# A trunk layer on one core: the first four column tiles take the input without its norm

## The chip, the core and the metric

The kernel runs on one core of one Trainium2 chip. The core has a matrix engine (TensorE, "PE" in the profile, with its weight loads as "PEld"), a vector engine (VectorE, "DVE"), a scalar engine that applies functions (ScalarE, "ACT"), GpSimd ("POOL") and a queue that issues the transfers (SyncE, "SP"). Each engine works through its own list of instructions in order, and waits where an instruction needs what another engine or a transfer has not yet delivered. The metric is the device time of one execution in microseconds (us); lower is better.

## What is computed

One layer works on 640 tokens of 1024 channels: 128 context tokens and 512 latent tokens. The part that the change touches is the first sub-layer's input:

```python
sh1, sc1, g1, sh2, sc2, g2 = split(silu(cond) @ w_ada + b_ada)      # per channel; cond: c_ctx for context, c for latent
h    = rmsnorm(x, norm1_g) * (1 + sc1) + sh1
proj = h @ w_in + b_in                                              # q, k, v, o, gates, u, ga, gb
```

`rmsnorm` multiplies each token by the reciprocal root of its mean square over the channels. The columns of `proj` feed a bidirectional mLSTM (q, k, v, o and the gate columns), a convolution branch (u, through a gated linear unit) and two branch gates; both branches are merged and projected, and a second sub-layer (norm, gated MLP with a depthwise convolution) and a final norm follow. All in float32.

## The kernel before

Activations lie transposed: channels on the 128 partitions, the 640 tokens along the free axis, so x is 8 tiles of 128x640 (index j). A column tile of `proj` is 128 output columns by 640 tokens and sums over the 8 channel tiles. For precision each float32 product is taken as three fast ones (`three`): every operand is split into a rounded high part and the rest, and high x high, low x high, high x low are summed in PSUM. Weights come in groups of 8 blocks of 128x128 (tile `wst`, 512 KB). ACT rounds such a group to `wh`, DVE subtracts to get `wl`. For the activations ACT makes `hh` and DVE makes `hl`.

The start runs like this. The 8 x tiles are loaded, then `ada1` weights (tiles `adst`, 16 loads of 512 KB) alternate with weight groups. ACT squares each x tile (`sq`), and PE sums the squares over the partitions (`colsum_into`, into a `ps` tile). `rstd` makes the reciprocal root (`rsy`), and `bcast` spreads it by PE over the partitions (kept as `rbs`). For each j the task `ada1` lets PE multiply the modulation weights with the condition (`ps<-adst,sc_pad`), ACT copies the row (`mrow`), PE turns it to columns (`ps<-sel,mrow`), and DVE makes the shift `mods` and the scale `a1`. The task `first_h(j)` then does, for tile j: on DVE x times `rbs`; on ACT `hh` = scale and shift of x, rounded; on DVE the same scale and shift in place; on DVE `hl`, the difference.

The first four column tiles (`FIRST`: two of u, the gate columns "g", the first of k) are computed together, j in the outer loop, so that a tile j can be used as soon as it is ready: 32 groups of three products, each over 256 and 384 tokens. Their sums occupy two `mm` tiles and two `ps` tiles of PSUM. After them come single tiles (`mtile`), beginning with q 0, k 1, q 1, u 1, each needing `hh` and `hl` of all 8 j. There are two `mm` tiles, so the third such tile needs the first one evicted.

Behind the first tiles ACT evicts: `gy` and `gt` (the gated unit), `gi` and `az` (the mLSTM's gates), `k`. DVE then runs the gates' scans (`bc`, `M`) and makes `pk` and `mj`, which PE transposes in the midst of tile u 1. The weights of the convolution (31 taps per tile, DVE), and later the modulation of the second sub-layer, are DVE work that is filled in wherever a place is free.

The order of each engine's list is set when the program is built: a small planner (`_Order`) keeps an estimated time for each engine, runs a task's next step when its inputs are estimated as ready, and so interleaves tasks (`od.spawn`, `yield`, `od.until`). On the chip the lists are fixed. All operations go through one helper, so every row of the profile has the same line, and one tells them apart by tile names.

## Time and profile before

| | |
|---|---|
| Time, median of 3 runs | 977.38 us (976.42 to 977.95) |
| The profiled execution's own time | 975.71 us |
| Its span (first to last instruction) | 973.5 us |
| PE busy | 946.8 us, 97% |
| DVE busy | 735.1 us, 76% |
| ACT busy | 362.2 us, 37% |
| POOL busy | 6.0 us, 1% |
| First matmul of the column tiles starts | 21.54 us |
| Last matmul of the first four tiles starts | 61.34 us |

A row of the timeline gives the start in us, the busy time in us, the engine, the operation with output and inputs by tile name and shapes, the number merged, and in brackets the idle time of the engine just before and who ended it. A row of the groups gives the count, the busy time in us and the mean of one in ns, and the idle time before. A row of the windows gives, for a stretch, the busy time (and count) of PE, PEld, DVE, ACT and POOL, then the granted TensorE clock, the busy share of the transfer engines, and GB/s.

### The profile page before, as it was taken

The page shows a single profiled execution, that of the slowest core. Times are in us where ns is not written, and L with a number is a line of the kernel's source. Part 1 is how long each engine was busy: PE and PEld are TensorE (multiplying, and loading weights), DVE is VectorE, ACT ScalarE, POOL GpSimd, SP SyncE. Part 2 cuts the span into 40 slices and gives each one's busy share as a digit, 9 for nine tenths or more (in the row PEclk, how much of TensorE's full clock was granted, in tenths as well). Part 3 has the DMA queues.
Part 4 walks back from the last instruction along what each step waited for, and adds up shares of the span by engine and source line. Part 5 has one row for each costly group of instructions (what it writes and reads, how often), then busy time and mean ns, then how long its engine had stood idle before and what let it go on. Part 6 is the DMA issues. An engine that isn't in the chain of part 4 may idle for free.

```text
span 973.5 us, 16460 instructions
## 1 busy us (share of the span) xinstructions
PE 946.8 (97%) x6700; PEld 924.2 (95%) x6700; DVE 735.1 (76%) x1348; ACT 362.2 (37%) x658; POOL 6.0 (1%) x41
## 2 busy tenths in 40 slices
...
GB/s 355 245 104 87 45 76 66 74 47 45 87 141 71 104 196 189 201 233 251 147 135 102 77 79 63 163 87 65 82 71 65 88 68 84 65 88 94 123 170 113
DMA packets 38971, 113.01 MB, mean 116 GB/s; under 512 B 4336, under 2 KB 7280, under 8 KB 38896
## 3 DMA queue, kind: packets, MB, share of 16 engines
...
q8 instruction: 53, 0.87, 0.4%
...
## 4 chain that ended last, share of the span: by engine, by line
PE 92%; DVE 4%; ACT 2%; issue 1%; DMA 1%; SPq 0%; DVEq 0%; ACTq 0%
PE mm L139 84%; PE ps L139 8%; DVE junk L139 1%; DVE acc L139 1%; DMA x<-in_xT 1%; DVE wl L139 0%; ACT wh L139 0%; ACT h L139 0%; ACT L139 0%; DVE rsy L139 0%; DVE yo L139 0%; ACT h2h L139 0%; DVE rst L139 0%; ACT sq L139 0%; SPq L139 0%
## 5 line engine op out<-in xcount | busy, mean ns | idle before, releaser
L139 ACT ACTIVATE wh<-wst 128x1024 fp32r<-128x1024 f32 x145 | 152.9, 1057 | 197.1 <-PE mm L139 166.8
L139 DVE TENSOR_TENSOR wl<-wst,wh 128x1024 fp32r<-128x1024 f32 x145 | 176.5, 1220 | 56.2 <-ACT wh L139 55.9
L139 PE MATMUL mm<-h2h,wl 128*128 128x320 f32 x704 | 164.9, 310 | 2.4 <-DVE wl L139 2.4
L139 PE MATMUL mm<-h2h,wh 128*128 128x320 f32 x704 | 165.0, 310 | 0.6 <-ACT h2h L139 0.6
L139 PE MATMUL mm<-h2l,wh 128*128 128x320 f32 x704 | 164.8, 310 | 0.4 <-DVE h2l L139 0.4
L139 PE MATMUL mm<-hh,wh 128*128 128x320 f32 (+2 forms) x576 | 134.3, 312 | 3.5 <-ACT wh L139 2.5
L139 PE MATMUL mm<-hl,wh 128*128 128x320 f32 (+2 forms) x576 | 133.7, 311 | 0.0
L139 PE MATMUL mm<-hh,wl 128*128 128x320 f32 (+2 forms) x576 | 133.4, 310 | 0.0
L139 DVE SCALAR_TENSOR_TENSOR acc<-gbuf,cols,acc 128x455 f32<-128x455 f32 (+2 forms) x176 | 129.7, 742 | 4.4
L139 PEld LDWEIGHTS mm<-h2h,wl 128*128 128x128 f32 x704 | 119.2, 189 | 2.8 <-DVE wl L139 2.7
L139 PEld LDWEIGHTS mm<-h2h,wh 128*128 128x128 f32 x704 | 119.3, 189 | 1.3 <-ACT h2h L139 1.2
L139 PEld LDWEIGHTS mm<-h2l,wh 128*128 128x128 f32 x704 | 119.1, 188 | 1.1 <-DVE h2l L139 1.0
L139 DVE SCALAR_TENSOR_TENSOR z<-glu,cols,z 128x641 f32<-128x641 f32 (+14 forms) x120 | 102.2, 889 | 0.8
L139 PEld LDWEIGHTS mm<-hh,wh 128*128 128x128 f32 x576 | 96.0, 188 | 5.8 <-ACT wh L139 3.0
L139 PEld LDWEIGHTS mm<-hl,wh 128*128 128x128 f32 x576 | 96.6, 188 | 2.2 <-issue 1.3
L139 PEld LDWEIGHTS mm<-hh,wl 128*128 128x128 f32 x576 | 96.9, 189 | 0.7 <-issue 0.7
L139 PE MATMUL mm<-ah,wl 128*128 128x320 f32 (+2 forms) x320 | 85.6, 308 | 0.0
L139 PE MATMUL mm<-ah,wh 128*128 128x320 f32 (+2 forms) x320 | 85.4, 307 | 0.0
L139 PE MATMUL mm<-al,wh 128*128 128x320 f32 (+2 forms) x320 | 85.4, 307 | 0.0
L139 DVE SCALAR_TENSOR_TENSOR junk<-ad,cb 128x512 bf16<-128x512 f32 x128 | 81.8, 686 | 0.1
L139 PEld LDWEIGHTS mm<-ah,wl 128*128 128x128 f32 x320 | 56.8, 188 | 0.1
L139 PEld LDWEIGHTS mm<-al,wh 128*128 128x128 f32 x320 | 56.8, 188 | 0.0
...
## 6 DMA issues: line engine op xcount, KB each, us to landing
wst<-in_w SPq DMA_DIRECT2D x145, 512.0 KB, 3.6
...
adst<-in_ada SPq DMA_DIRECT2D x16, 512.0 KB, 10.2
x<-in_xT SPq DMA_DIRECT2D x16, 320.0 KB, 5.7
...
```

The lines of the kernel that those rows point to most:

```text
L139: return fn(*args, **kw)
```

## The change

The first four column tiles no longer take the normed input. A new task `scaled(j)` makes, as soon as x tile j and its modulation are there, g = x times `a1` (scale only, no norm), with two columns more that hold the shift of both conditions (642 columns), and splits it: `gh` on ACT, `gl` on DVE (a ring of 6 tiles, `NFG`). `FIRST` is computed on g. When the sums leave PSUM, `first_out` multiplies them on DVE with `rbs` (the norm is one factor per token, so it may be applied behind the product) into an SBUF tile `fo`, copies the two columns that the shift gave (`fs`), and adds those on ACT. The tiles that follow read `fo` in place of PSUM.

The normed input for all other tiles is made by a task `normed`: for each j on DVE g times `rbs` in place, on ACT `hh` = g plus the shift, rounded, on DVE the shift added in place, on DVE `hl`. The sum of squares is a task `norm1`: ACT squares, GpSimd adds the eight tiles up, PE sums once over the partitions (4 matmuls where there were 32). The loads go by turns: `cols`, modulation weights of j = 0, x 0, `sel`, a weight group, x 1, and so on; the bytes are the same.

The lists move as follows. PE at its start (`sq` are squares, `adst` modulation weights, `rsy` the norm, `mm` the first tiles); before:

```order
L139 MATMUL ps<-sq,ones_83 32x160 x32
L139 MATMUL ps<-adst,sc_pad 32x256 x8
L139 MATMUL ps<-rsy,sel 128x160 x4
L139 MATMUL ps<-sel,mrow 128x128 x2
L139 MATMUL ps<-adst,sc_pad 32x256 x8
L139 MATMUL mm<-hh,wh 128x256
```

and now:

```order
L140 MATMUL ps<-adst,sc_pad 32x256 x8
L140 MATMUL ps<-sel,mrow 128x128 x2
L140 MATMUL mm<-gh,wh 128x256
L140 MATMUL mm<-gh,wh 128x386
L140 MATMUL mm<-gl,wh 128x256
L140 MATMUL mm<-gl,wh 128x386
L140 MATMUL mm<-gh,wl 128x256
L140 MATMUL mm<-gh,wl 128x386
L140 MATMUL ps<-adst,sc_pad 32x256 x8
```

The sums of squares and the broadcast of the norm, which stood ahead of the first tile, have gone behind its beginning; one modulation product stands ahead of it instead of two.

DVE around the normed input, in the part of the first four tiles; before (tile j, then the next, with the modulation and a weight group between):

```order
L139 TENSOR_TENSOR x<-x,rbs 128x640 [waits DMAHW6_49]
L139 TENSOR_SCALAR x<-x,a_211,mods 128x128 [waits Activation_49]
L139 TENSOR_SCALAR x<-x,a_211,mods 128x512 [waits Activation_49]
L139 TENSOR_TENSOR hl<-x,hh 128x640 [waits DVE_49]
```

and now, beginning with the weights of j = 4 and 5 (each row with what it waits for):

```order
L140 TENSOR_TENSOR wl<-wst,wh 128x1024 [waits DMAHW2_49]
L140 TENSOR_TENSOR g<-g,rbs 128x640
L140 TENSOR_SCALAR g<-g,mods 128x128 [waits Activation_49]
L140 TENSOR_SCALAR g<-g,mods 128x512 [waits Activation_49]
L140 TENSOR_TENSOR hl<-g,hh 128x640 [waits DVE_49]
L140 TENSOR_SCALAR a_156<-ps,sc1p,cols 128x2 [waits PE_49]
L140 TENSOR_SCALAR mods<-ps,cols 128x2
L140 TENSOR_SCALAR g<-x,a_156 128x128 [waits DMAHW3_49,DVE_49]
L140 TENSOR_SCALAR g<-x,a_156 128x512
L140 COPY g<-mods 128x2 [waits DVE_49]
L140 TENSOR_TENSOR gl<-g,gh 128x642 [waits DVE_49,PE_49,Activation_49]
L140 TENSOR_TENSOR wl<-wst,wh 128x1024 [waits DMAHW5_49]
```

Here normed tile 0 stands ahead of the modulation and of `gl` for j = 7 and of the weights for j = 6 and 7; three weight groups, normed tiles 1 and 2, the twelve rows that take the four tiles out of PSUM (`fo`, `fs`) and then normed tiles 3 to 7 follow, four rows each, one tile behind the other.

ACT where the evictions of the first tiles begin; before:

```order
L139 ACTIVATE wh<-wst 128x1024 [waits DMAHW7_49,PE_49,Activation_49]
L139 ACTIVATE gy<-mm,halfc 128x256 [waits PE_49]
L139 ACTIVATE gy<-mm,halfc 128x384
L139 ACT_TABLE_LOAD
L139 ACTIVATE gt<-mm,halfc 128x256
```

and now:

```order
L140 ACTIVATE fo<-fo,fs 128x512
L140 ACTIVATE hh<-g,mods 128x128 [waits DVE_49,Pool_49]
L140 ACTIVATE hh<-g,mods 128x512
L140 ACTIVATE gy<-fo,halfc 128x640 [waits Activation_49]
L140 ACT_TABLE_LOAD
L140 ACTIVATE gt<-fo,halfc 128x640 [waits Activation_49]
L140 ACTIVATE gi<-fo,cols 64x640 [waits Activation_49]
```

The pair of `hh` rows stands there five times, for j = 3 to 7, and `gy` with all that follows it comes behind the last of them.

The diff, cut to its core:

```diff
--- before.py
+++ after.py
@@ -68,6 +68,7 @@
 MARGIN = 0.0
 NFST = 256
 NAD1 = 6
+NFG = 6
 NST = 3
 NWT = 3
 
@@ -518,15 +519,14 @@
 
 
     x = []
-    for j in range(KD):
-        t = A([P, T], name="x")
-        Q.dma_start(t, xT[j])
-        x.append(t)
-        if j == 3:
-            Q.dma_start(cols, cols_d)
-    Q.dma_start(sel, sel_d)
-
+    fg = first.enter_context(tc.tile_pool(name="fg", bufs=NFG))
     adst = {}
+
+    def x_load(*js):
+        for j in js:
+            t = A([P, T], name="x")
+            Q.dma_start(t, xT[j])
+            x.append(t)
 
     def ada1_load(j):
         t = [adp.tile([P, 4, 256], F32, tag="ad1", name="adst") for _ in range(2)]
@@ -534,22 +534,24 @@
             Q.dma_start(t[i], ada1_d[j, :, 4 * i:4 * i + 4, :])
         adst[j] = t
 
+    Q.dma_start(cols, cols_d)
     ada1_load(0)
+    x_load(0)
+    Q.dma_start(sel, sel_d)
     load(0)
+    x_load(1)
     ada1_load(1)
+    x_load(2, 3)
     ada1_load(2)
+    x_load(4, 5)
     load(1)
-    for j in range(3, NAD1):
+    ada1_load(3)
+    x_load(6, 7)
+    for j in range(4, NAD1):
         ada1_load(j)
-    pc = ps()
-    for j in range(KD):
-        sq = A([P, T], name="sq")
-        S.activation(sq, x[j], AF.Square)
-        if j == 3:
-            th = small([P, 16], "th")
-            S.activation(th, colr("c"), AF.Tanh, scale=0.5)
-            sqrt_table()
-        colsum_into(pc, sq, bgrp, j == 0, j == KD - 1)
+    th = small([P, 16], "th")
+    S.activation(th, colr("c"), AF.Tanh, scale=0.5)
+    sqrt_table()
     V.scalar_tensor_tensor(th, th, 1.0, colr("c"), op0=ALU.add, op1=ALU.mult)
     sc_pad = cp.tile([P, KD, 32], F32, name="sc_pad")
     V.memset(sc_pad, 0.0)
@@ -566,8 +568,6 @@
         V.tensor_scalar(halfc[:, o:o + b - a], cols[:, a:b], 0.5, None, op0=ALU.mult)
         HC[nm] = o
         o += b - a
-
-    r1 = rstd(pc[:, 0:bgrp], bgrp, 1.0 / D, "rs")
 
     def hcol(name, i):
         return halfc[:, HC[name] + i:HC[name] + i + 1]
@@ -597,54 +597,110 @@
             for i in range(2):
                 PE.matmul(pm[:, 128 * i:128 * i + 128], lhsT=mrow[:, 128 * i:128 * i + 128], rhs=adasel,
                           start=True, stop=True)
-            V.tensor_scalar(mods[:, j, :], pm[:, 0:2], col("b_ada", j), None, op0=ALU.add)
             V.tensor_scalar(a1[:, j, :], pm[:, 128:130], sc1p[:, j:j + 1], col("norm1_g", j),
                             op0=ALU.add, op1=ALU.mult)
-            t_h.append(od.spawn(first_h(j)))
-
-    def first_h(j):
+            V.tensor_scalar(mods[:, j, :], pm[:, 0:2], col("b_ada", j), None, op0=ALU.add)
+            t_g.append(od.spawn(scaled(j)))
+
+    CTX_LAT = ((0, slice(0, NCTX)), (1, slice(NCTX, T)))
+    g_, gs = [], []
+
+    def scaled(j):
+
+        g = A([P, T + 2], name="g")
+        g_.append(g)
+        gh, gl = (fg.tile([P, T + 2], F32R, tag="fg", name=n) for n in ("gh", "gl"))
+        gs.append((gh, gl))
+        for c, s in CTX_LAT:
+            S.activation(gh[:, s], x[j][:, s], AF.Identity, scale=a1[:, j, c:c + 1])
+        S.activation(gh[:, T:T + 2], mods[:, j, :], AF.Copy)
+        for c, s in CTX_LAT:
+            V.tensor_scalar(g[:, s], x[j][:, s], a1[:, j, c:c + 1], None, op0=ALU.mult)
+        V.tensor_copy(g[:, T:T + 2], mods[:, j, :])
+        V.tensor_sub(gl, g, gh.bitcast(F32))
+        yield
+
+    def norm1():
+
+        for j in range(KD):
+            yield from od.until(x[j])
+            sq = A([P, T], name="sq")
+            S.activation(sq, x[j], AF.Square)
+            if j == 0:
+                total = sq
+            else:
+                G.tensor_add(total, total, sq)
+        yield from od.until(total)
+        pc = ps()
+        colsum_into(pc, total, bgrp, True, True)
+        r1 = rstd(pc[:, 0:bgrp], bgrp, 1.0 / D, "rs")
+        yield from od.until(r1)
+        rb = bcast(r1, bgrp)
+        t = A([P, T], name="rbs")
+        for h in range(2):
+            S.activation(t[:, HALF[h]], rb[h], AF.Copy)
+        rbs.append(t)
+
+    def normed():
+
         while not rbs:
             yield
-        if j == 0:
-            for h in range(2):
-                V.tensor_mul(x[j][:, HALF[h]], x[j][:, HALF[h]], rb[h])
-        else:
-            V.tensor_mul(x[j], x[j], rbs[0])
-        hh, hl = A([P, T], F32R, "hh"), A([P, T], F32R, "hl")
-        hs.append((hh, hl))
-        yield
-        for c, s in ((0, slice(0, NCTX)), (1, slice(NCTX, T))):
-            S.activation(hh[:, s], x[j][:, s], AF.Identity, scale=a1[:, j, c:c + 1], bias=mods[:, j, c:c + 1])
-        for c, s in ((0, slice(0, NCTX)), (1, slice(NCTX, T))):
-            V.tensor_scalar(x[j][:, s], x[j][:, s], a1[:, j, c:c + 1], mods[:, j, c:c + 1], op0=ALU.mult, op1=ALU.add)
-        V.tensor_sub(hl, x[j], hh.bitcast(F32))
-
-    t_h = []
+        yield from od.until(rbs[0])
+        for j in range(KD):
+            while len(g_) <= j:
+                yield
+            yield from od.until(g_[j])
+            yield from od.room("V")
+            g = g_[j]
+            V.tensor_mul(g[:, 0:T], g[:, 0:T], rbs[0])
+            yield
+            hh, hl = A([P, T], F32R, "hh"), A([P, T], F32R, "hl")
+            for c, s in CTX_LAT:
+                S.activation(hh[:, s], g[:, s], AF.Identity, bias=mods[:, j, c:c + 1])
+            for c, s in CTX_LAT:
+                V.tensor_scalar(g[:, s], g[:, s], mods[:, j, c:c + 1], None, op0=ALU.add)
+            V.tensor_sub(hl, g[:, 0:T], hh.bitcast(F32))
+            hs.append((hh, hl))
+            yield
+
+    t_g = []
     rbs = []
     mrows = []
     t_ada = od.spawn(ada1())
-    while not mrows:
+    od.spawn(norm1())
+    t_hs = od.spawn(normed())
+    pu = [mm_ps(), mm_ps()]
+    pl = [ps()[:, 0:T + 2 - NFST] for _ in range(2)]
+    pu = [[(pu[i // 2][:, 0, NFST * (i % 2):NFST * (i % 2 + 1)], slice(0, NFST)),
+           (pu[i // 2][:, 1, 0:T + 2 - NFST] if i % 2 == 0 else pl[i // 2], slice(NFST, T + 2))] for i in range(4)]
+    for j in range(KD):
+        while len(t_g) <= j:
+            od.finish_one()
+        od.finish(t_g[j])
+        for i, (nm, m) in enumerate(FIRST):
+            three(pu[i], W((nm, j, m)), gs[j], j == 0, j == KD - 1, shared=1 + i % 2)
+    od.finish(t_ada)
+
+    def first_out(i):
+
+        f = A([P, T], name="fo")
+        (p0, s0), (p1, s1) = pu[i]
+        V.tensor_mul(f[:, s0], p0, rbs[0][:, s0])
+        V.tensor_mul(f[:, NFST:T], p1[:, 0:T - NFST], rbs[0][:, NFST:T])
+        sh = sm.tile([P, 2], F32, tag="fs", name="fs", bufs=4)
+        V.tensor_copy(sh, p1[:, T - NFST:T + 2 - NFST])
+        for c, s in CTX_LAT:
+            S.activation(f[:, s], f[:, s], AF.Identity, bias=sh[:, c:c + 1])
+        return [(f, slice(0, T))]
+
+    while not rbs:
         od.finish_one()
-    rb = bcast(r1, bgrp)
-    t = A([P, T], name="rbs")
-    for h in range(2):
-        S.activation(t[:, HALF[h]], rb[h], AF.Copy)
-    rbs.append(t)
-    pu = [mm_ps(), mm_ps()]
-    pl = [ps()[:, 0:T - NFST] for _ in range(2)]
-    pu = [[(pu[i // 2][:, 0, NFST * (i % 2):NFST * (i % 2 + 1)], slice(0, NFST)),
-           (pu[i // 2][:, 1, 0:T - NFST] if i % 2 == 0 else pl[i // 2], slice(NFST, T))] for i in range(4)]
-    for j in range(KD):
-        while len(t_h) <= j:
-            od.finish_one()
-        od.finish(t_h[j])
-        for i, (nm, m) in enumerate(FIRST):
-            three(pu[i], W((nm, j, m)), hs[j], j == 0, j == KD - 1, shared=1 + i % 2)
-    od.finish(t_ada)
+    first_outs = [first_out(i) for i in range(len(FIRST))]
+    od.finish(t_hs)
     first.close()
 
     def tile_of(nm, m):
-        return pu[FIRST.index((nm, m))] if (nm, m) in FIRST else mtile(nm, m, range(KD), hs)
+        return first_outs[FIRST.index((nm, m))] if (nm, m) in FIRST else mtile(nm, m, range(KD), hs)
 
 
     def glu(m):
```

## The prediction

> **What bounds the kernel now.** I read the page's span and chain first, then the busy time by stage, then the timeline of the first 90 us, where the change lies.
>
> ```profile
> span 973.5 us, 16460 instructions
> PE 92%; DVE 4%; ACT 2%; issue 1%; DMA 1%; SPq 0%; DVEq 0%; ACTq 0%
> ...
> 0.00:10.00 10.00, 3.04 (x32) 0.81 (x32) 1.36 (x14) 5.94 (x9) 0.57 (x14) 1.00 0.80 273
> 10.00:22.00 12.00, 7.92 (x79) 3.73 (x80) 5.29 (x13) 6.45 (x12) 0.14 (x2) 1.00 1.03 413
> 22.00:37.00 15.00, 15.00 (x129) 11.02 (x127) 10.49 (x22) 6.21 (x13) 3.55 (x17) 0.89 1.03 408
> 37.00:62.00 25.00, 24.68 (x187) 23.04 (x186) 16.16 (x33) 10.83 (x16) 0.00 (x0) 1.00 0.39 132
> 62.00:100.00 38.00, 37.39 (x251) 35.76 (x252) 32.45 (x59) 19.78 (x37) 0.44 (x6) 1.00 0.35 62
> 100.00:440.00 340.00, 338.49 (x2447) 334.02 (x2446) 302.88 (x642) 131.01 (x273) 0.00 (x0) 1.00 0.35 114
> ```
>
> PE makes 92% of the chain. It idles 11 us before 22 us and hardly at all after, so what it gains or loses before 100 us reaches the end whole. DVE is the second resource: 33 of 62 us busy at first, then 85 to 89%.
>
> ```profile
> 21.54 0.58 PE L139 MATMUL mm<-hh,wh 128*128 128x256 f32 x2 [2.53 <-ACT wh L139]
> 25.72 0.28 PE L139 MATMUL mm<-hh,wh 128*128 128x256 f32 x1
> ...
> 53.69 0.28 PE L139 MATMUL mm<-hh,wh 128*128 128x256 f32 x1
> 54.57 0.45 PE L139 MATMUL mm<-hh,wh 128*128 128x256 f32 x2
> ...
> 61.34 0.33 PE L139 MATMUL ps<-hh,wl 128*128 128x384 f32 x1
> 62.61 0.56 PE L139 MATMUL mm<-hh,wh 128*128 128x320 f32 x2 [0.93 <-ACT gt L139]
> ...
> 47.99 0.83 DVE L139 TENSOR_TENSOR hl<-x,hh 128x640 fp32r<-128x640 f32 x1
> ```
>
> The first four tiles run from 21.54 to 61.5 us. One group of three products takes 0.88 (53.69 to 54.57), 32 take 28.2. From 25.72 on, 31 groups (27.3) leave 8.5 us for five modulation products and six column products, 1.55 a pair. The last normed half (`hl`, 47.99) is done 13 us before q 0 needs it, so the normed input costs PE nothing today: that is the cover to watch.
>
> **The change, part by part.** *Start.* Ahead of the first group now stand `cols` (128x487), two modulation loads, x 0, `sel`, a weight group and x 1 (ACT squares x 1 before it rounds the weights).
>
> ```profile
> wst<-in_w SPq DMA_DIRECT2D x145, 512.0 KB, 3.6
> adst<-in_ada SPq DMA_DIRECT2D x16, 512.0 KB, 10.2
> x<-in_xT SPq DMA_DIRECT2D x16, 320.0 KB, 5.7
> ...
> L139 ACT ACTIVATE sq<-x 128x640 f32<-128x640 f32 x8 | 5.5, 728 | 3.3 <-DMA x<-in_xT 3.2
> ```
>
> That is 2.6 MB (page's list of loads); at 273 GB/s (first row of the stages) 9.7 us, about 10.7 with landing. Square (0.7) and rounding (1.05) put the first product at 12.6; bounds 11.6 (no landing time) and 14.6 (modulation at the slow clock below). Later loads are hidden: the group for j = 4 has 11.9 MB before its end, 32 us, and ACT comes to it at about 41.
>
> *The four tiles.* The work from 12.6 on is more than before, since what stood ahead now stands inside: 28.2 for the groups, seven pairs 10.9, the sum of squares 0.7 (was eight such), the broadcast 1.2 (1.35 busy, its end overlapped), and the slow clock:
>
> ```profile
> 10.56 2.64 PE L139 MATMUL ps<-sq,ones 128*32 128x160 f32 x32 [1.49 <-ACT sq L139]
> 16.21 1.35 PE L139 MATMUL ps<-rsy,sel 128*128 128x160 f32 x8 [0.88 <-DVE rsy L139]
> 22.00:23.00 1.00, 1.00 (x9) 0.78 (x11) 1.00 (x1) 0.00 (x0) 0.00 (x0) 0.50 0.99 401
> 25.00:26.00 1.00, 1.00 (x6) 1.00 (x7) 0.00 (x0) 1.00 (x2) 0.02 (x1) 0.82 1.01 401
> ```
>
> The granted clock is 0.50 from 22 for some 3.6 us once the dense stretch begins, a loss of 1.8, paid again. Sum 42.8: 55.4 without a wait, 6 us early. But the lists have five waits. Weight halves: 1.2 behind the first group and 1.2 at j = 2 (ACT has `gh` and two squares ahead of the rounding). The sum of squares waits for GpSimd: ACT's last squares stand behind `mrow` of j = 3 (PE's product for it at 28), end at 30, and two of the seven adds follow.
>
> ```profile
> 26.77 0.63 POOL L139 MEMSET bc<- 64x640 f32 x1 [1.75 <-PE ps L139]
> ```
>
> An add of 640 columns is not in this trace. Below, a GpSimd fill of 640, 0.63; above, three streams of that, 1.9; I take 1.25 (it moves more than a fill), a wait of 1.0, bounds 0 and 2. The Trainium skill, "GPSIMD Engine Reference", 3.1 (side-by-side), has such an add at 1.96 times VectorE's time: by that and the 0.82 of a DVE row below, an estimate of 1.6, and 0.7 more of wait. No run here shows it yet.
>
> Fourth, DVE has `wl` of j = 4 behind `gl` of j = 6. PE comes to the columns of j = 6 at 42.8 (12.6 + 13.8 + six pairs 9.3 + 0.7 + 1.2 + 1.8 + 3.4 waits); then scale 0.3, `gh` 1.1, `gl` 0.8, `wl` 1.2: 46.2, and PE waits 2.5. Fifth, `wl` of j = 6 stands behind normed tile 0 (below): 1.2 more. So the four tiles end at about 62.5, against 61.5: **the early start is used up.**
>
> *The normed input* is what decides. Each tile is a chain over two engines, since the in-place addition on DVE must wait until ACT has read g, and DVE has nothing else in its list meanwhile. Tile 0 of before shows it:
>
> ```profile
> 18.37 0.87 DVE L139 TENSOR_TENSOR x<-x,ps 128x320 f32<-128x320 f32 x2
> 19.36 1.19 ACT L139 ACTIVATE hh<-x,mods,a 128x128 fp32r<-128x128 f32 x2
> 19.88 0.35 DVE L139 TENSOR_SCALAR x<-x,a,mods 128x128 f32<-128x128 f32 x1 [0.63 <-ACT hh L139]
> 20.58 0.55 DVE L139 TENSOR_SCALAR x<-x,a,mods 128x512 f32<-128x512 f32 x1 [0.35 <-ACT hh L139]
> 21.90 1.22 DVE L139 TENSOR_TENSOR wl<-wst,wh 128x1024 fp32r<-128x1024 f32 x1
> ...
> L139 DVE TENSOR_SCALAR kw<-kq,ca 128x128 f32<-128x128 f32 x32 | 7.6, 281 | 0.7 <-PE ps L139 0.7
> L139 ACT ACTIVATE hf<-hf,hry 128x128 f32<-128x128 f32 x20 | 6.5, 390 | 0.0
> L139 ACT ACTIVATE hh<-x,mods,a 128x128 fp32r<-128x128 f32 x8 | 3.9, 485 | 1.2 <-DVE x L139 1.2
> L139 DVE TENSOR_TENSOR x<-x,rbs 128x640 f32<-128x640 f32 x7 | 5.7, 816 | 0.0
> L139 DVE TENSOR_TENSOR va<-mm,vb 128x256 f32<-128x256 f32 x10 | 4.2, 420 | 1.2 <-PE mm L139 1.2
> L139 DVE TENSOR_TENSOR qp<-q,ps 128x512 f32<-128x512 f32 x8 | 5.5, 686 | 2.7 <-PE ps L139 2.7
> ```
>
> From 18.37 to the next DVE operation at 21.90 it is 3.5 us, the upper bound. With one operand per partition for two, an ACT part is 0.1 shorter (485 to 390), two of them 0.2, and a DVE part 0.07 (the 0.35 at 19.88 to 281), and one product of 640 (816) replaces two (0.87): 3.1, which I take. Below, 2.5 if ACT's 1.0 were mostly hidden.
>
> From 46.2: g times `rbs` to 47.0; ACT is not free, as it holds `mrow` of 7 (PE's product after the wait: 48.2) and two weight groups, to 50.3; `hh` 0 to 51.3, addition and `hl` to 52.6; then scale, `gh`, `gl` of j = 7 to 54.8 and three `wl` to 58.3, normed tiles 1 and 2 to 64.5. The four tiles leave PSUM with 256 (0.42) and 384 columns (between 0.42 and 0.69) and a copy each, 4.1 in all: 68.6. Five chains of 3.1: **84.1**. PE starts q 0 at about 66.5, when its PSUM tile is free, has three tiles of the input, then gets one per 3.1 us and uses it up in 0.88; q 0 ends at 84.7, before at 62.61 + 7.04 = 69.65: **+15.0**.
>
> *Behind it*, ACT's `gy` stands after the last `hh` (82.8), and the gates' chain after that, where it began at 59.83 before.
>
> ```profile
> 59.83 0.94 ACT L139 ACTIVATE gy<-mm,halfc 128x256 f32<-128x256 f32 x2 [4.24 <-PE mm L139]
> 66.88 0.74 ACT L139 ACTIVATE az<-az 64x640 f32<-64x640 f32 x1
> 72.90 2.36 DVE L139 TENSOR_TENSOR wl<-wst,wh 128x1024 fp32r<-128x1024 f32 x2
> 81.94 0.82 DVE L139 TENSOR_TENSOR mj<-bc,M 64x640 f32<-64x640 f32 x1
> 86.44 0.27 PE L139 MATMUL ps<-sel,pk 128*128 128x128 f32 x1
> ```
>
> `gy` to the last `az` was 7.8, now 7.2 (no split in two by PSUM): 90.0. From there to the end of `mj` was 15.1, now 14.8 (no tap, one weight group more): 104.8. PE gets `wl` of the third tile at 96.5 and is at the transposes at 104.1; they wait to 104.8, before 86.44: **+18.4**. From here the lists hold the same work, PE binds, and nothing is given back. I add 1.6 for the slow clock in the half-idle stretch (0 to 3.6, twice 1.8) and for DVE's later start on its taps (0 to 4).
>
> Sum: span 973.5 + 20 = 993.5; with the 2.2 around it (975.71 - 973.5) 995.7; the median of the runs lies 1.7 above the profiled run: **997 us**.
>
> **The rivals.** *Faster:* DVE keeps pace. Its rows up to the last `hl` are about 48 us busy (eight times 2.0 for g, eight times 2.1 for the normed input, six weight groups 7.2, the norm 2.5, leaving PSUM 4.1, 1.5 at first); from 9.6 without a wait that ends at 57.7. The tiles end at 55.4, q 0 starts at 57.5 against 62.61: -5.1, 972 us. It decides at some 10 us of DVE idle up to the last `hl`; for it speaks that the planner set this order by its own times, against it that each chain alone waits 1.0 and ACT and PE hold the list at j = 4 to 7; I count 26. *Half as slow:* eight chains of 2.5 (-4.8), no wait for GpSimd (-1), the start 1 us early (-1), 2 of the other waits gone: +11, 988 us. For it speaks that I added up every wait of the lists, against it the row of 3.5. *Slower still:* the stretch from 66 to 97, where PE works 0.88 of 3.1 us, leaves it at clock 0.50 and every resumption pays 1.8; both come in full, the landing is late by 2 and DVE's backlog costs 4 at the next norm: +28, 1005 us. The Trainium skill, "TensorE: Matmul & The Clock Gate", Part 1, says that the array runs at half rate after an idle window until about 3.4 us of sustained work; the rows at 22 and 25 agree. By that rule alone 2 us are added to my sum, since the first resumption hides behind `wl` of the third tile. *No effect:* the waits just eat the start, as at 62.5, and the input is ready: 977 us; it would need the last `hl` by about 69.
>
> **How the numbers follow.** Forecast (+14 to +24) 0.62, half as slow 0.14, slower still 0.14, faster 0.07, no effect 0.03. Its own bounds: start -1 to +2, chains -4.2 to +2.8, GpSimd -1 to +1, other waits -3 to +2, clock and backlog -1.6 to +6. They rarely fall together, so 984 to 1007, which takes in most of the rivals on its own side. This kernel's runs tell 0.2% (2 us) from no change: faster 0.07, within 0.03, slower 0.90.
>
> **What would show it.** First product at 11.6 to 14.6; the four tiles' end near 62.5; DVE rows of g times `rbs` 3.1 us apart behind the `fo` rows, with idle ended by ACT `hh`; the last `hl` near 84; PE idle some 18 us between 62 and 100, ended by DVE `hl`, `wl` or ACT; the same PE time as before from the transposes on. I am wrong if DVE is not idle between its addition rows, if the last `hl` comes before 72, or if PE's idle time lies elsewhere.

## The result and the profile after

The changed kernel takes 1003.63 us (median of 6 runs, 999.92 to 1006.09) against 976.90 us (6 runs, 974.33 to 977.95): 1.0274 times the time before, 95% interval 1.0247 to 1.0302. It is slower by 26.7 us. The profiled execution took 1006.09 us, 30.4 more than that of before, so offsets read from the trace are some 4 us larger than those of the medians.

The page of the changed kernel (span, and the shares of the chain of waits):

```profile
span 1004.3 us, 16459 instructions
...
PE 86%; DVE 5%; DMA 3%; ACT 3%; issue 1%; SPq 0%; DVEq 0%; ACTq 0%
```

The changed kernel in the stages used for before, from 10 to 100 us, by windows:

```profile
10.00:22.00 12.00, 8.58 (x56) 6.33 (x60) 5.51 (x13) 5.85 (x12) 3.15 (x2) 1.00 1.02 402
22.00:37.00 15.00, 12.91 (x108) 10.73 (x104) 9.03 (x14) 6.75 (x15) 8.88 (x5) 0.89 1.02 417
37.00:62.00 25.00, 22.30 (x167) 18.54 (x160) 16.28 (x38) 11.70 (x25) 0.00 (x0) 0.86 0.12 34
62.00:100.00 38.00, 28.86 (x139) 24.80 (x137) 28.00 (x54) 21.96 (x36) 4.24 (x33) 0.78 0.20 63
```

PE's share of the chain falls from 92 to 86%. From 22 to 62 us PE was idle for 0.3 us before and is now for 4.8, at a granted clock of 0.89 and then 0.86 (before 0.89 and 1.00); from 62 to 100 it is idle for 9.1 (before 0.6) at 0.78 (before 1.00). GpSimd is busy for 12 us within the first 37 (before 4.3).

The timeline of PE, changed kernel:

```profile
14.24 0.90 PE L140 MATMUL mm<-gh,wh 128*128 128x256 f32 x2 [3.08 <-ACT wh L140]
16.84 1.61 PE L140 MATMUL ps<-adst,sc_pad 128*32 128x256 f32 x16
...
29.88 0.56 PE L140 MATMUL mm<-gh,wl 128*128 128x256 f32 x2 [1.66 <-DMA adst<-in_ada]
49.45 0.91 PE L140 MATMUL mm<-gh,wl 128*128 128x256 f32 x2 [2.71 <-DVE wl L140]
67.37 0.34 PE L140 MATMUL ps<-gh,wl 128*128 128x386 f32 x1
71.26 0.53 PE L140 MATMUL mm<-hh,wh 128*128 128x320 f32 x2 [3.56 <-DVE fo L140]
...
102.16 0.57 PE L140 MATMUL mm<-hh,wl 128*128 128x320 f32 x2 [2.41 <-DVE wl L140]
113.48 0.27 PE L140 MATMUL ps<-sel,pk 128*128 128x128 f32 x1
```

The column tiles begin 7.3 us earlier than before (14.24 for 21.54), yet the last product of the four starts 6.0 us later (67.37 for 61.34), and the transposes of `pk` come 27.0 us later (113.48 for 86.44).

The timeline of DVE over the normed input, changed kernel:

```profile
76.81 0.82 DVE L140 TENSOR_TENSOR g<-g,rbs 128x640 f32<-128x640 f32 x1
78.15 0.28 DVE L140 TENSOR_SCALAR g<-g,mods 128x128 f32<-128x128 f32 x1 [0.53 <-ACT hh L140]
78.77 0.49 DVE L140 TENSOR_SCALAR g<-g,mods 128x512 f32<-128x512 f32 x1 [0.33 <-ACT hh L140]
...
80.03 0.82 DVE L140 TENSOR_TENSOR g<-g,rbs 128x640 f32<-128x640 f32 x1
...
88.90 0.83 DVE L140 TENSOR_TENSOR hl<-g,hh 128x640 fp32r<-128x640 f32 x1
...
109.61 0.82 DVE L140 TENSOR_TENSOR mj<-bc,M 64x640 f32<-64x640 f32 x1
```

The chain is there as read from the lists: the rows of g times `rbs` are 3.2 us apart, with DVE idle for 0.53 and 0.33 until ACT has read g. The last `hl` ends at 89.7.

Two rows stand at the same place of every kernel's list and serve as marks from here on: the last product of the branch gates (`gb<-gb,mm`) and the last row by which the first sub-layer is added to x. Before, from DVE's timeline:

```profile
431.10 0.81 DVE L139 SCALAR_TENSOR_TENSOR gb<-gb,mm 128x640 f32<-128x640 f32 x1
488.79 0.55 DVE L139 SCALAR_TENSOR_TENSOR x<-mm,g1h,x 128x320 f32<-128x320 f32 x1 [0.24 <-PE mm L139]
```

and after:

```profile
457.52 0.82 DVE L140 SCALAR_TENSOR_TENSOR gb<-gb,mm 128x640 f32<-128x640 f32 x1
519.99 0.54 DVE L140 SCALAR_TENSOR_TENSOR x<-mm,g1h,x 128x320 f32<-128x320 f32 x1
```

The first mark is 26.4 us late, the second 31.2: some 26 us are lost by about 120 us and kept, and another 4.8 are lost between 457 and 520 us, far from the change.

### The profile page after: what moved, and what is told of

The parts are those of the page before. It is cut to its first block, busy times and chain, and to the rows that moved or that the text cites. A ratio compares the mean times of both kernels' runs of the same rounds, so it can differ in the third digit from the quotient of the medians.

```text
span 1004.3 us, 16459 instructions
## 1 busy us (share of the span) xinstructions
PE 960.0 (96%) x6644; PEld 936.3 (93%) x6644; DVE 755.4 (75%) x1390; ACT 373.0 (37%) x685; POOL 17.9 (2%) x48
## 4 chain that ended last, share of the span: by engine, by line
PE 86%; DVE 5%; DMA 3%; ACT 3%; issue 1%; SPq 0%; DVEq 0%; ACTq 0%
PE mm L140 80%; PE ps L140 7%; DMA adst<-in_ada 2%; DVE wl L140 1%; DVE acc L140 1%; DVE g L140 1%; DMA wst<-in_w 1%; ACT hh L140 1%; SPq L140 0%; DVE hl L140 0%; ACT h L140 0%; DVE junk L140 0%; ACT h2h L140 0%; ACT wh L140 0%; ACT fo L140 0%
## 5 line engine op out<-in xcount | busy, mean ns | idle before, releaser
L140 PE MATMUL mm<-hh,wh 128*128 128x320 f32 x528 | 124.6, 318 | 5.9 <-DVE fo L140 3.6
L140 PE MATMUL mm<-hl,wh 128*128 128x320 f32 x528 | 124.5, 318 | 3.0 <-DVE hl L140 3.0
L140 PE MATMUL mm<-hh,wl 128*128 128x320 f32 x528 | 124.7, 318 | 2.4 <-DVE wl L140 2.4
L140 DVE SCALAR_TENSOR_TENSOR z<-glu,cols,z 128x641 f32<-128x641 f32 (+14 forms) x120 | 102.2, 889 | 0.7
L140 PEld LDWEIGHTS mm<-hh,wh 128*128 128x128 f32 x528 | 89.9, 193 | 8.6 <-issue 4.3
L140 PEld LDWEIGHTS mm<-hl,wh 128*128 128x128 f32 x528 | 89.7, 192 | 5.1 <-DVE hl L140 4.7
L140 PEld LDWEIGHTS mm<-hh,wl 128*128 128x128 f32 x528 | 90.2, 193 | 3.3 <-DVE wl L140 2.7
L140 PEld LDWEIGHTS mm<-ah,wh 128*128 128x128 f32 x320 | 56.7, 188 | 0.0
```

The source lines that it names most:

```text
L140: return fn(*args, **kw)
```

## The experiments

All runs in one table: median, ratio to the kernel before (95%), start of the last product of the first four tiles, and how late the two marks are against before.

| kernel | us | ratio | last product of the four | mark `gb` | mark x |
|---|---|---|---|---|---|
| before | 976.90 | | 61.34 | | |
| after | 1003.63 | 1.0247 to 1.0302 | 67.37 | +26.4 | +31.2 |
| sums on TensorE | 999.29 | 1.0224 to 1.0257 | 61.98 | +19.3 | +24.2 |
| dead adds on GpSimd | 1003.36 | 1.0248 to 1.0313 | 64.12 | +23.8 | +29.4 |
| multiply ahead | 995.14 | 1.0178 to 1.0224 | 67.90 | +19.3 | +24.1 |
| no second split | 989.15 | 1.0117 to 1.0151 | 64.66 | +7.5 | +11.7 |
| second load of x earlier | 1000.63 | 1.0236 to 1.0271 | 66.81 | +25.9 | +26.8 |
| three mends | 990.78 | 1.0132 to 1.0166 | 62.54 | +17.3 | +17.3 |
| change with the old loads | 999.57 | 1.0228 to 1.0259 | 67.66 | +20.2 | +25.0 |
| before with the new loads | 989.98 | 1.0126 to 1.0162 | 74.58 | +12.8 | +12.8 |
| chain free | 978.44 | 1.0007 to 1.0026 | 60.23 | +3.2 | +3.5 |
| two more tiles on g | 986.18 | 1.0086 to 1.0116 | 60.37 | +12.5 | +12.5 |
| old loads, one more tile | 987.84 | 1.0069 to 1.0144 | 65.16 | +8.6 | +8.3 |
| weights ahead of the chain | 991.58 | 1.0127 to 1.0186 | 60.66 | +19.0 | +19.5 |

The last three columns come from one profiled execution of each kernel, which is not always near the median: it lies 2.5 us above it for after, 3.5 above for multiply ahead, 2.4 above for three mends, 1.8 above for second load of x earlier and 4.3 below for no second split; for the others it lies within 1.6. The first product also starts anywhere from 12.36 to 14.24 in executions with the new loads, so that differences of 1 to 2 us at the end of the four tiles can be that alone. The intervals of after, sums on TensorE, change with the old loads and second load of x earlier overlap: what is said of those 3 to 4 us rests on the traces.

**Sums on TensorE.** The sum of squares goes back to PE, as before the change; all else stays.

```diff
-            if j == 0:
-                total = sq
-            else:
-                G.tensor_add(total, total, sq)
-        yield from od.until(total)
+            sqs.append(sq)
+        yield from od.until(*sqs)
...
-        colsum_into(pc, total, bgrp, True, True)
+        for j in range(KD):
+            colsum_into(pc, sqs[j], bgrp, j == 0, j == KD - 1)
```

> The changed kernel, but the eight tiles of squares are summed by TensorE (eight times four products into one PSUM tile, together, once the eighth is there), as before the change, and GpSimd adds nothing. Theory, that the GpSimd adds cost twice (they end late, at 35.8 us, and VectorE's g pair took 1.4 to 2.0 us beside them where it takes 0.67 alone, wl 1.7 to 2.5 where it takes 1.22): the sums are there 2 to 4 us earlier, the four tiles end at 64 to 65 in place of 67.5, the time is about 1000.5 (998 to 1002). Rival, that all this is covered because the last ada tile lands at 37 us either way: the tiles' end stays within 1 us and the time at 1003.6 +- 1.5. Second rival, that 32 small products (about 5 us of TensorE) stand in front of products that could run: slower, about 1007.

Measured: 999.29 us, inside what I expected, and the four tiles' last product starts at 61.98, 5.4 earlier than after and earlier than I expected. Of these 5.4, 0.8 are there at the first product (13.40 for 14.24), which the adds do not touch. The adds cost more than the wait that I had given them. The timeline of the changed kernel, DVE beside an add of GpSimd:

```profile
26.52 2.23 POOL L140 TENSOR_TENSOR sq<-sq 128x640 f32<-128x640 f32 x1 [0.67 <-ACT sq L140]
24.64 1.69 DVE L140 TENSOR_SCALAR g<-x,a 128x128 f32<-128x128 f32 x2
27.35 2.47 DVE L140 TENSOR_TENSOR wl<-wst,wh 128x1024 fp32r<-128x1024 f32 x1
```

and in the experiment:

```profile
23.91 0.67 DVE L140 TENSOR_SCALAR g<-x,a 128x128 f32<-128x128 f32 x2
26.61 1.23 DVE L140 TENSOR_TENSOR wl<-wst,wh 128x1024 fp32r<-128x1024 f32 x1 [0.75 <-ACT wh L140]
```

The same operations take twice as long or more while GpSimd adds. `wl` ends at 29.82, and the row of PE at 29.88, which the profile puts down to a transfer (`adst`), follows it by 0.06: the wait was for `wl`. Behind both of its long waits PE is then on a slower clock. The changed kernel by microseconds (stretch, its length, PE, PEld, DVE, ACT, POOL, clock, transfers):

```profile
32.00:33.00 1.00, 1.00 (x6) 1.00 (x5) 0.00 (x0) 1.00 (x2) 0.35 (x1) 0.50 1.07 438
...
49.00:50.00 1.00, 0.55 (x2) 0.50 (x2) 1.00 (x2) 0.00 (x0) 0.00 (x0) 0.50 0.00 0
```

and the experiment, where the wait for `wl` of j = 4 was 1.07:

```profile
48.00:49.00 1.00, 0.57 (x4) 0.57 (x5) 1.00 (x5) 0.00 (x0) 0.00 (x0) 1.00 0.00 0
```

Around the waits of 1.66 and 2.71 us the clock falls to 0.50, until 35 and until 55.5; with the one of 1.07 it stays at 1.00. That this wait is shorter is not the contention's doing: in the experiment PE has 2.38 us of sums ahead of it in place of 0.48, and the planner has put the modulation of j = 7 ahead of it too; with the adds running again (next run) it is 1.07 as well. So the 5.4 us are not the contention alone.

**Dead adds on GpSimd.** The sums stay on PE, and GpSimd makes as many adds into a tile that nobody reads. This was meant to keep the contention and to take away the lateness of the sum.

```diff
+            sqs.append(sq)
             if j == 0:
-                total = sq
+                dead = A([P, T], name="dead")
+                G.memset(dead, 0.0)
             else:
-                G.tensor_add(total, total, sq)
-        yield from od.until(total)
+                G.tensor_add(dead, dead, sq)
+        yield from od.until(*sqs)
```

> The squares are summed by TensorE, as in the run before with that edit, and GpSimd runs its seven additions all the same, into a tile that nobody reads. It parts the two costs of the GpSimd sums: that they run beside VectorE, and that they end late. Theory, that VectorE beside GpSimd is what moved the four tiles' end by 5 us (g pair 0.67 to 1.4 to 2.0, wl 1.22 to 1.7 to 2.5): the tiles end at 65 to 67 again and the time is 1002 to 1005. Rival, that the late sums (rbs at 41.8 us) and the normed tiles that stand behind them did it: the tiles end at 62 to 63 with VectorE's rows slow all the same, and the time is 999 to 1000.5.

Measured: 1003.36 us, as in the first theory, with the last product at 64.12, between the two: 2.1 later than with the sums on PE alone (0.5 of it there at the first product). The marks are 4.5 and 5.2 later. The timeline of the experiment, first GpSimd, then DVE and PE:

```profile
32.67 3.45 POOL L140 TENSOR_TENSOR dead<-dead,sq 128x640 f32<-128x640 f32 x2 [3.92 <-ACT sq L140]
34.63 1.51 DVE L140 COPY g<-mods 128x2 f32<-128x2 f32 x1
36.99 0.32 DVE L140 TENSOR_SCALAR rsv<-ps 128x160 f32<-128x160 f32 x1
29.88 0.56 PE L140 MATMUL mm<-gh,wl 128*128 128x256 f32 x2 [1.60 <-DMA adst<-in_ada]
```

A copy of two columns, which the changed kernel elsewhere does in 0.16, takes 1.51 us, and ends (36.14) where the second of the two adds ends (36.12). The Trainium skill, "Perfetto Trace Analysis", Optimizing Scalar/DVE Operations, says that GpSimd and DVE share an SBUF read port, so that moving work between them might not help; this run agrees as far as the delay goes, since 1.5 us is about one whole add.

The run does not part the two costs as it was meant to. The norm is as late as after: its first row on DVE (`rsv`) starts at 36.99, after at 37.25, and with the sums on PE alone at 34.67, since the sums now stand in PE's list behind the same slowed rows. So the 3.2 us that still lie between this run and after at the end of the four tiles are not the late sum. They arise behind the wait for `wl` of j = 4 (1.07 here, 2.71 after): from there to the last product it is 13.6 us here and 17.9 after, where the clock is at 0.50 until 55.5 and the modulation of j = 7 is still to come.

It also holds a counterexample on the clock. The wait at 29.88 is 1.60 us, as long as after (1.66), and no slow clock follows. The window behind it:

```profile
30.00:35.00 5.00, 5.00 (x70) 3.98 (x74) 1.98 (x5) 2.75 (x6) 2.25 (x2) 1.00 1.02 419
```

A wait of that length is thus followed by the slow clock in one execution and not in another.

**Multiply ahead.** g times `rbs` of the next tile is put into DVE's idle time before the additions.

```diff
-        for j in range(KD):
+        def scale(j):
...
+            V.tensor_mul(g_[j][:, 0:T], g_[j][:, 0:T], rbs[0])
+
+        yield from scale(0)
+        for j in range(KD):
...
-            V.tensor_mul(g[:, 0:T], g[:, 0:T], rbs[0])
-            yield
...
+            if j + 1 < KD:
+                yield from scale(j + 1)
+            yield
```

> The changed kernel, but each normed tile's multiplication by rbs is issued ahead of the additions of the tile before it, so that VectorE has work while ScalarE makes hh. Theory, that the normed inputs are one serial chain of 3.2 us a tile of which VectorE works 2.4: five chains behind the fo rows take 12 us instead of 16, the last hl ends at about 85.5 instead of 89.7, and gl of tile 7 no longer stands behind the additions of tile 0, which waited 4.75 us for hh: another 2 us. Time about 997.5 (995 to 1000). Rival, that ScalarE is the bound there (hh pairs of 1.0 us, eight fo rows of 3.7 us and the gates' rows behind them): the last hl still ends at 88 or later and the time stays at 1002 to 1004.

Measured: 995.14 us. DVE's timeline of the experiment:

```profile
74.95 0.82 DVE L140 TENSOR_TENSOR g<-g,rbs 128x640 f32<-128x640 f32 x1
75.68 0.68 DVE L140 TENSOR_SCALAR g<-g,mods 128x128 f32<-128x128 f32 x2
...
77.14 0.82 DVE L140 TENSOR_TENSOR g<-g,rbs 128x640 f32<-128x640 f32 x1
```

The chains are 2.2 us apart for 3.2, DVE waits for nothing between them, and the last `hl` ends at 83.1 for 89.7. The mark `gb` gains 7.1. What I expected at the end of the four tiles did not come: 67.90, no earlier than after. That the rows of the normed input set the pace behind the four tiles is shown.

**No second split.** The tiles after the first four take g as well; the normed input with its split is not made, so norm and shift are left out of those tiles' products.

```diff
-        for j in range(KD):
...
-            V.tensor_mul(g[:, 0:T], g[:, 0:T], rbs[0])
...
-            V.tensor_sub(hl, g[:, 0:T], hh.bitcast(F32))
-            hs.append((hh, hl))
+        while len(gs) < KD:
+            yield
+        hs.extend(gs)
```

> The changed kernel without the second split: no input tile is normed again, and all later column tiles take the products of x and a as they are (the norm and the shift are left out of them, so this measures what the chain costs and computes something else). Theory, that the chain of normed inputs behind the four tiles is most of the loss: TensorE goes on at 71 us and the first q leaves PSUM at about 80 instead of 97, the time falls by about 17 to 986 (983 to 990), and what stays of the loss is the first stage (6), the wait for the fo rows (2.6) and the late stall (4). Rival, that the loss sits in the first 67 us, in the waits for wl and in the clock, and the chain is mostly covered by products: 997 or more.

Measured: 989.15 us. The mark `gb` is 7.5 late instead of 26.4, 19 us less; but this profiled execution took 984.89 us where the three others took 989.1 to 989.3. By the medians the normed input as a second, later product of DVE carries 14.5 of the 26.7 us, which is the safer figure. PE's timeline of the experiment:

```profile
64.83 0.46 PE L140 MATMUL mm<-gh,wh 128*128 128x320 f32 x2
```

This is tile q 0, 0.17 behind the last product of the four: PE goes on without a wait, where the changed kernel waits 3.56 us for `fo`. A second loss, the one behind 457 us, stays (4.3 between the marks).

**Second load of x earlier.** The late loss comes from transfers. SP's issues after:

```profile
459.84 0.33 SPq L140 DMA_DIRECT2D ad<-in_ada  x1
460.22 4.03 SPq L140 DMA_DIRECT2D x<-in_xT  x8
```

and before:

```profile
429.06 0.33 SPq L139 DMA_DIRECT2D ad<-in_ada  x1
429.44 3.76 SPq L139 DMA_DIRECT2D x<-in_xT  x8
```

In both, x is loaded anew behind a load of modulation weights (`ad`) that waits for a place which DVE frees by its `junk` rows. The first row that adds to x starts at 437.28 before, 7.8 us behind the issue, and at 463.71 after, only 3.5 us behind it: the planner has put the `junk` that frees the place one branch tile later (it ends 2.1 us ahead of the last `gb` row before, and 2.3 behind it after). Weights queue behind x, and PE waits for them, after:

```profile
472.99 0.42 PE L140 MATMUL mm<-mgh,wh 128*128 128x320 f32 x1 [2.27 <-ACT wh L140]
```

The experiment moves the eight loads of x ahead by two branch tiles.

```diff
+    x2 = []
...
+        if (nm, m) == ("b", 6):
+            for i in range(8):
+                t = A([P, T], name="x2")
+                Q.dma_start(t, xT[i])
+                x2.append(t)
...
-    x2 = []
-    for m in range(8):
-        t = A([P, T], name="x2")
-        Q.dma_start(t, xT[m])
-        x2.append(t)
```

> The changed kernel, but the eight loads of x for the residual stand on the queue ahead of the ada load that waits 7.0 us for VectorE's junk (one branch tile earlier in the program). Theory, that the 4 us lost at 464 to 480 us come from the planner having put that wait in front of eight x loads and three weight loads: the x rows at 465 us no longer wait for their loads, the weight tile lands 3 to 4 us earlier, TensorE does not stop at 472, and the time is 999.2 (998 to 1000.5). Rival, that the weight load is late by itself (its buffer comes free late): the stop stays, and the time is 1003 or more.

Measured: 1000.63 us, just above the theory's range. In SP's timeline of the experiment the loads leave at 451.80:

```profile
451.80 3.94 SPq L140 DMA_DIRECT2D x<-in_xT  x8
```

Between the marks 0.9 us are lost, after lost 4.8. The medians (3.0 us apart) have intervals that overlap, so it is the trace that settles this, not the time. Its first stage has the list of after, and there the timeline of PE shows another thing:

```profile
35.51 0.48 PE L140 MATMUL ps<-sq,ones 128*32 128x160 f32 x8 [1.41 <-POOL sq L140]
```

PE waits 1.41 us for GpSimd's sum. It had waited 1.62 for `wl` at 29.23, with the clock at 1.00 behind it; in the profiled execution of after the slow clock stands in that place and hides the wait for the sum.

**Three mends.** The three edits above (sums on TensorE, multiply ahead, second load earlier) together:

```diff
+            sqs.append(sq)
...
+            if j + 1 < KD:
+                yield from scale(j + 1)
...
+        if (nm, m) == ("b", 6):
```

> The changed kernel with three mends together: squares summed by TensorE, each normed tile's multiplication ahead of the additions before it, the second loads of x ahead of the waiting ada load. Theory, that the three remove different waits (the first stage's, VectorE's wait inside the chain, the stop at 472 us): 4.3 + 8.5 + 3.0 of the separate medians nearly add up, a little less because the chain then starts earlier and both touch it: 988 (985 to 991), still about 11 slower than before the change, since five tiles of the chain still stand behind the fo rows with TensorE waiting. Rival, that the first two remove the same idle time of VectorE: 992 or more.

Measured: 990.78 us, at the edge of what I expected, and no sum of its parts: the mark `gb` gains 9.1, where the two edits ahead of it gained 7.1 each alone. With DVE faster, PE waits 3.31 us at 92.04 for a `wl` that stands behind the chains.

**Change with the old loads.** All x tiles first, as before the change, so that the norm is there early and the first product late.

```diff
-NAD1 = 6
-NFG = 6
+NAD1 = 5
+NFG = 8
...
+    x_load(0, 1, 2, 3)
     Q.dma_start(cols, cols_d)
-    ada1_load(0)
-    x_load(0)
+    x_load(4, 5, 6, 7)
     Q.dma_start(sel, sel_d)
+    ada1_load(0)
```

> The changed kernel with the loads in the order from before the change (all x first, then ada; one ada tile fewer in flight and one more pair of gh, gl buffers, for room). The first product comes some 6 us later (about 20 us), the sums of squares are there 10 us earlier. Theory, that the loads fill the queue until 37 us in either order and TensorE's start is not what sets the end: the four tiles end at 66 to 69 as now and the time is 1000 to 1006. Rival, that the early start is worth its 6 us: 1008 or more. Other rival, that the late sums cost more than the early start brings: 998 or less.

Measured: 999.57 us, 4 us less than after. PE's timeline of the experiment:

```profile
23.04 0.76 PE L140 MATMUL ps<-sq,ones 128*32 128x160 f32 x8 [6.16 <-POOL sq L140]
25.26 0.90 PE L140 MATMUL mm<-gh,wh 128*128 128x256 f32 x2 [1.46 <-ACT wh L140]
```

The column tiles begin 11.0 us later than after (I had expected 6), since PE's product for the sums stands ahead of them and waits 6.16 us for GpSimd. Yet their last product starts only 0.3 later (67.66). So in the changed kernel the early start was worth nothing where the four tiles end. Behind them the old order is even better: the norm is there sooner, the last `hl` ends at 83.5 for 89.7, and the marks gain 6.2.

**Before with the new loads.** The kernel before, with only the order of its loads changed.

```diff
-    for j in range(KD):
-        t = A([P, T], name="x")
-        Q.dma_start(t, xT[j])
...
+    Q.dma_start(cols, cols_d)
     ada1_load(0)
+    x_load(0)
+    Q.dma_start(sel, sel_d)
     load(0)
+    x_load(1)
     ada1_load(1)
+    x_load(2, 3)
```

> The kernel before the change with the changed order of the loads alone (x and ada by turns; the first four tiles still take the normed x). It tells what part of the change's first product the order of loads is worth by itself. Theory: the norm needs the last x, which now lands at about 27 us instead of 12, so the products start some 12 us later while the modulation is done early; TensorE has 28 us of four-tile products left behind that: the four tiles end at 68 to 72 instead of 61.5, time about 985 (982 to 990). Rival, that the last ada tile at 37 us sets the end in both orders: 976 to 979.

Measured: 989.98 us. PE's timeline of the experiment:

```profile
34.79 0.73 PE L139 MATMUL mm<-hh,wh 128*128 128x256 f32 x2 [2.53 <-ACT wh L139]
```

The column tiles begin 13.25 us later than before, and 12.8 us of it are there at both marks. The time is at the top of what I expected and the four tiles end later (74.58 for 68 to 72). Where the first tiles need the norm, the new order of loads only costs.

**Chain free.** Sums on TensorE, second load earlier and no second split at once: the change without the three things found to cost.

```diff
-                G.tensor_add(total, total, sq)
+            sqs.append(sq)
...
-            V.tensor_sub(hl, g[:, 0:T], hh.bitcast(F32))
-            hs.append((hh, hl))
+        while len(gs) < KD:
+            yield
+        hs.extend(gs)
...
+        if (nm, m) == ("b", 6):
```

> An upper bound on what the early start can bring: no input tile is normed again (the norm and the shift are left out of all products but those of the first four tiles, as in the run without the second split), the squares are summed by TensorE, and the second loads of x stand ahead of the waiting ada load. Nothing of the three costs that the runs found is left. Theory, that TensorE has the same work up to the four tiles' end in either order (50.5 us before, 50.3 with the sums on TensorE) and idles 11 to 12 us for the first loads in both, so that the early product only changes places with other work: the tiles end at 61 to 62.5 and the time is 977 to 982, not faster than before even so. Rival, that the early start is worth something once the costs are gone: the tiles end before 60 and the time is 973 or less.

Measured: 978.44 us (10 runs, 977.35 to 979.26), 1.0016 times before: no gain, even with work left out (norm and shift are missing in the later tiles' products). The four tiles end at 60.6, just ahead of the range that I gave. PE's timeline of the experiment:

```profile
13.44 0.90 PE L140 MATMUL mm<-gh,wh 128*128 128x256 f32 x2 [3.08 <-ACT wh L140]
...
60.41 0.45 PE L140 MATMUL mm<-gh,wh 128*128 128x320 f32 x2
78.07 0.56 PE L140 MATMUL mm<-gh,wl 128*128 128x320 f32 x2 [2.85 <-DVE wl L140]
```

Tile q 0 begins at 60.41 (before 62.61), and a wait of 2.85 for weights, with the clock at 0.50 behind it for some 3 us, takes that back. These weights are late by the change's own way out of PSUM: the `fo` rows stand ahead of `gy`, which begins at 63.32 (before 59.83), and the pair of `wl` behind the gates begins at 76.79 (before 72.90). Why 8.1 us of earlier start shrink to 2.2 stands in two windows of the experiment:

```profile
0.00:14.00 14.00, 3.94 (x22) 1.92 (x23) 3.84 (x21) 6.67 (x11) 0.58 (x14) 1.00 0.87 312
14.00:37.00 23.00, 22.18 (x222) 16.86 (x224) 10.04 (x26) 9.97 (x21) 0.00 (x0) 1.00 1.03 417
```

and of before:

```profile
0.00:14.00 14.00, 6.49 (x72) 1.85 (x72) 1.67 (x16) 8.72 (x13) 0.57 (x14) 1.00 0.87 314
14.00:37.00 23.00, 19.48 (x170) 13.71 (x166) 15.48 (x34) 9.88 (x20) 3.69 (x19) 0.93 1.03 409
```

By 37 us PE has been busy for 26.1 us in the one and 26.0 in the other. The idle time ahead of the first product was not idle time of the stage: sums, modulation and broadcast of the norm lay there and now lie inside.

**Three versions meant to gain.** With the mends, one or two more tiles take g as the first four do, so that PE has work while the normed input is made. The first, with q 0 and k 1 on g (its core):

```diff
+EXTRA = [('q', 0), ('k', 1)]
...
+    def extra_tile(nm, m):
+        pt = mm_ps()
+        outs = [(pt[:, 0, 0:TH], slice(0, TH)), (pt[:, 1, 0:T + 2 - TH], slice(TH, T + 2))]
+        for k in range(KD):
+            three(outs, W((nm, k, m)), gs[k], k == 0, k == KD - 1)
+        return first_out(outs)
```

> The three mends, and two more column tiles (q 0 and k 1) take x without its norm and are scaled and shifted on leaving PSUM like the first four, so that TensorE has 15 us of products while the chain of normed inputs runs (gh and gl of all eight tiles are kept for that). Theory, that the chain costs only because nothing stands beside it: the four tiles end at 62.3, the fo rows cost 1 to 2, and then TensorE runs on without a stop, so that the first q 1 product finds its inputs: 978.5 (976 to 982), about what the kernel before takes. Rival, that the four tiles cannot gain anything and two more fo rounds on VectorE and ScalarE push the gates and the weights back: 984 or more. Other rival, that the earlier first product counts now: 974 or less.

Measured: 986.18 us; the rival was right. PE has no wait from 28 to 82 us, and then, in its timeline, among others these:

```profile
84.53 0.56 PE L141 MATMUL mm<-hh,wl 128*128 128x320 f32 x2 [1.94 <-DVE wl L141]
93.83 0.90 PE L141 MATMUL mm<-hh,wh 128*128 128x320 f32 x2 [2.57 <-ACT q L141]
```

DVE's work has not shrunk. That its rows for `fo` and the normed input push back the weights and the evictions is my reading of these two waits; no run tries it alone. The second version keeps one such tile and takes the old loads:

```diff
-NAD1 = 6
+NAD1 = 5
...
+EXTRA = [('q', 0)]
...
+    x_load(0, 1, 2, 3)
```

> The three mends, the loads in the order from before the change, and one more column tile (q 0) that takes x without its norm. With x first the sums and rbs are there by about 30 us, so five of the eight normed tiles can be made before the four tiles end, and q 0 covers the other three. Theory, that the time follows TensorE's own work: the first product comes at 20 to 25 us, later than in the change by 6 to 11, and the four tiles still end at 62 to 64; behind them TensorE stops for less than 3 us up to 100 us, and the time is 979 (976 to 983), within 0.7 % of the kernel before. Rival, that the early first product is what the change gains by: the tiles end at 68 or later and the time is 988 or more. Other rival, that the gates and weight halves behind the chain stop TensorE at 80 to 100 us as with two more tiles: 984 to 987.

Measured: 987.84 us, 9 above what I expected; PE waits 3.13 us for `wl` at 90.81, and behind the second mark, where it is 8.3 late, its span of 986.7 (13.2 above before) shows another 5: at 633.70 PE waits 5.36 for a `wl`, where before it waits 2.44 (622.58), which is 2.9 of them; the rest was not traced. The third puts the weights of the tiles that follow ahead of the rest of the chain:

```diff
+        extras.append(extra_tile(nm, m))
+        W((("k", 0, 1), ("q", 0, 1), ("u", 0, 1))[len(extras) - 1])
+        chain_to(KD)
```

> The kernel with two more column tiles, and the halves of the next two weight loads issued ahead of the rest of the chain instead of behind it. In the run with two more tiles TensorE stood still or waited at 84.5 (wl, 1.9 us), 93.8 (q on ScalarE, 2.6 us) and 97.4 us (wl, 2.1 us). Theory, that what is left of the loss is these waits behind the chain: the wl wait at 84.5 goes, the one at 97.4 shrinks, the time falls by 2 to 4 to 983 (981 to 985). Rival, that the waits only move to the next row, because VectorE is busy without a gap from 60 to 100 us: 985.5 to 988.

Measured: 991.58 us, above what either theory gave. The waits have only moved: 4.79 us for ACT (`q`) at 96.12 and 4.75 for DVE (`va`) at 112.56. No kernel here is faster than the one before.

## Why the prediction was right, and where it was not

Slower, by the mechanism named and inside the range; the time was forecast 997 and is 1003.63. Its steps against the trace:

| step | forecast | measured |
|---|---|---|
| first product | 12.6 (11.6 to 14.6) | 14.24; 12.36 to 14.24 in executions with these loads |
| wait for the sums of squares | 1.0 (0 to 2) | none; 1.07 and 1.41 in two experiments with GpSimd's adds |
| end of the four tiles | 62.5 | 67.6 |
| add of 640 columns on GpSimd | 1.25 (below 1.9) | median 1.58, 2.23 beside `wl` |
| distance of the chains | 3.1 (2.5 to 3.5) | 3.2 |
| last `hl` | 84.1 | 89.7 |
| `wl` of the third tile | 96.5 | 102.2 |
| end of `mj` | 104.8 | 110.4 |
| transposes | 104.8 | 113.5 |
| PE idle from 62 to 100 | some 18 | 9.1, at clock 0.78 |
| lateness at the transposes | +18.4, with clock and backlog +20 | +27.0, then +26.4 kept |
| behind the transposes | nothing | +4.8 |

**What held.** The early start is used up; the normed input decides; its chains are 3.2 us apart; the distance from the last `hl` to the end of `mj` (20.7 forecast, 20.7 measured) is right to a tenth, and the fourth wait (2.5 forecast, 2.71) nearly. *Multiply ahead* and *no second split* confirm it: the one fills DVE's idle time in the chains and gets back 8.5 us of the median, the other leaves the step out and gets back 14.5. The rival *faster* is out: from 9.6 us to the last `hl` DVE was busy for 52.1 of 80.1 us and idle for 28.0, where the rival allowed 10 and I had counted 26. PE's loss between 62 and 100 us is where I had it, but half in another form: 9.1 us of idle time, and a granted clock of 0.78 for the rest.

**The step that failed: "So the four tiles end at about 62.5".** It came 5.1 us later, and every later time carries that. By terms: the first product 1.6 late; the waits 5.1 (0.33, 0.43, 1.66, 2.71; the one for the sums and the fifth did not come) where the step had 7.1, so -2.0; the slow stretches 6.6 where it had 1.8, so +4.8; the rest, by difference, +0.7. I had one slow stretch, at the start. There were three. The first group takes 2.60 us (14.24 to 16.84) with 0.33 of wait where 0.88 is the full pace, and the modulation products behind it 1.54 (to 18.38) for 1.00: 1.9 lost, though the rows of the clock read 1.00. Then, by the rows of the clock, 1.7 from 31 to 35 and 3.0 from 49.45 to 55.5. I had priced the wait for `wl` at its length and not at what PE does behind it. The stretch from 31 is partly chance: *second load of x earlier* has the same list there, no slow clock, a wait of 1.41 for the sums instead, and its four tiles end 0.6 earlier.

Under it lies the term for GpSimd's adds, "a wait of 1.0, bounds 0 and 2". In this execution PE never waited for the sums. The adds cost in another place, by stretching DVE's rows: `wl` took 1.25 longer, and PE waited 1.66 behind it. Taking the adds away moved the end of the four tiles by 5.4 us (0.8 of it from an earlier first product, and a part from the changed list) and the median by 4.3. I had priced an add by its duration and its place in the order, and not by what it does to DVE's rows beside it. The Trainium skill's ratio, "GPSIMD Engine Reference", 3.1, quoted in the prediction, gave 1.6 for an add, and the trace has a median of 1.58; the longer wait that I worked out from it is not where the cost lay.

Also, `gl` of j = 7 ended at 59.1 where I had 54.8, since `hh` of tile 0 came late (DVE waited 4.75 us for it at 54.88; ACT had waited 4.89 for PE's product of j = 7 ahead of it). The list was read rightly, and the times in it were early by the same slow stretch of PE.

**"They wait to 104.8"** was wrong in what PE waits for. `mj` ended at 110.43, and PE came to the transposes only at 113.48. What held it was `wl` of the third tile, at 102.16 (a wait of 2.41). From there it needs 11.3 us, where the step had 7.6: 33 pairs of products at 0.293 are 9.7, which before's list, with 31 pairs there, would have told (9.1), and the clock was at 0.50 for some 3.4 us behind the wait.

**"From here the lists hold the same work, PE binds, and nothing is given back"** was wrong by the 4.8 us of the second load of x. The planner's estimates shift with the change, and it arranged the lists at 450 us otherwise.

**The range held** since the rival *slower still* (1005) was in it, and in part by luck. Of its three parts the late landing (1.6) and the slow clock were there, though the clock cost most inside the four tiles and not, as that rival had it, only between 66 and 97. The third, 4 us at the next norm, did not come (behind the second mark, +31.2, nothing is lost: the span is 30.8 longer). The 4.8 us of the second load, for which the sum had no term, stand in its place.

**Why the early start brought nothing** is shown by *chain free* for its order of the lists: without the second split, without GpSimd's adds and without the late loss the kernel is 0.16% above before. What is left of the change there buys 2.2 us at the start of q 0 and pays for it with the `fo` rows on DVE and ACT, behind which the gates and the next weights come later. The change as it was built adds 8 more splits on both engines. That no order of the lists could keep the 2.2 us is not shown; three orders meant to gain did not.

**What stays open.** *Three mends* gains less than its parts (12.9 us of 15.8 by the medians); the 3.31 us wait for `wl` is one reason, the rest was not taken apart. How much of the loss by the adds is contention and how much the order of the lists stays open too, since each edit moved the lists as well. So does why the clock fell behind one wait of 1.6 us and not behind another.
